# Low parts from PSUM, later prompt rows, adaLN sums on four column groups and attention outputs scaled during the scan: four edits to a one-layer diffusion step

## The chip, the cores and the metric

One core of one Trainium2 chip runs the whole step. Its engines are TensorE (PE; its weight loads stand apart as PEld), VectorE (DVE), ScalarE (ACT), GpSimd (POOL) and SyncE (SP, which here only issues transfers). The metric is the device time of one execution in microseconds; lower is better.

## The reference, cut to what matters

The layer works on 1024 latent tokens and 256 prompt tokens of width 1024:

```python
sh1, sc1, g1, sh2, sc2, g2 = split(silu(cond) @ w_ada + b_ada, 6)   # adaln, for c and for c_ctx
h = rms_norm(x, norm_mix_w) * (1.0 + sc1) + sh1
z = h @ w_in                      # hq, hf_f, hf_b, hi, hg, aq, ak, av, gl
o_a = softmax(q k^T) v            # 8 heads of 64, block by block; q, k normalised, rotary for latents
o_h = two gated recurrent scans (hgrn), forward and backward, 4 heads of 128
merged = g[0] * (o_h @ w_ho) + g[1] * (o_a @ w_ao)
x = x + g1 * (merged @ w_out)
h = rms_norm(x, norm_ffn_w) * (1.0 + sc2) + sh2
x = x + g2 * (square(relu(h @ w_ff1)) @ w_ff2)     # then a final rms_norm
```

Prompt tokens use the modulation of `c_ctx`, latent tokens that of `c`. All products are wanted in float32.

## The kernel before

**Products.** A float32 product is made of three matmuls: both operands are split into a high part (rounded to the format `fp32r`) and a low part (the rest), and high x high, high x low and low x high are summed in PSUM. ACT makes high parts, DVE makes low parts.

**Tiles.** Tokens come in three tiles `t`: 0 and 1 are latent (512 each), 2 is the prompt (256). The channels of the width come in 8 chunks `kc` of 128.

**Order.** PE's instructions run in the order in which the program writes them. For the other engines a scheduler orders the instructions by simulating the program, with priorities and with `issue_after` (not before a named instruction). Each engine, and SP's transfer queue too, then works strictly in its order.

**Stages.** Up to about 100 us is the front. It computes the first 16 of the 48 column chunks of the modulation (`front_ada`). `norm1_rows(t)` loads rows `xr` of x, squares and sums them (tile `sq` on ACT, `sqv` on DVE), makes the factor `rst` (on DVE tile `mm`, then a power on POOL) and scales the rows on DVE (`f(0)`, `f(1)`, L279). `norm1_tr` transposes them on PE into PSUM tile `ps_t` (L285). `norm1_col` applies the modulation: ACT writes the high part `hs` (L297); the full value `xnb` is made by ACT (L302), or by DVE where `kc % 3 == 1` (L300); DVE subtracts the high part from it to get the low part (L303). `front_z` (L644 to L650) multiplies with the weights of k, v and half of q, in 24 steps (t, kc) counted by `idx`. The transposes run some steps ahead of the products: the last ones of latent tile 1 and the first ones of the prompt stand side by side in PE's order.

Attention follows, from about 138 to 690 us. Between its blocks a filler `fz` feeds PE with groups of projections for the scan: ten groups, in two rounds `zh(0)` and `zh(1)` of hq, hf, hf, hi, hg. Then comes the scan (`hgrn`, to about 985 us; 24 units, `i` counts them) with a filler `fg` of eight groups for the merge gates, and then the transition: attention outputs `OA` and scan outputs `OH` are loaded again from DRAM (tile `or`), the attention outputs are multiplied with the reciprocal softmax sums (`RS`, loaded as broadcast rows, L1337), all are split (L313) and projected (L345 to L347). The rest, from about 1030 us, is the merge, the output projection and the feed-forward layers.

**The rest of adaLN.** The other 32 column chunks are computed two at a time beside the fillers. `ada_sum` lets POOL multiply and add the rows (into `ACC`, shown as `sums` and `pvt`), and PE then only sums over the partitions (L210); nine calls, one in each group of `fz` but the first. `ada_cols` does it all on PE in four column groups of 32 (L178), copies the sums by ACT into `ev` and transposes them (L184); seven calls in `fg`. PSUM tile `ps_t` has two buffers, which attention's transposes (L877) share; the weight tile `wraw` has two as well, and SP's ring of tiles (`or`, `xr` and the scan's loads among them) twenty.

Of the kernel before, what the change touches and what calls it, by code (L numbers as in the profile page):

```python
# [44 lines left out]
def build(ctx, tc, I, O, C):  # L45
# [147 lines left out]
    def ada_sum(ci, acc):  # L193

        raw = wraw(I["w_ada"], KC, ci * P)
        w = [ada_l[:, :, c:c + 1].broadcast_to([P, KC, 256]) for c in range(2)]
        g_.tensor_tensor(acc[0], raw[:, 0], w[0][:, 0], op=ALU.mult)
        for k in range(1, KC):
            g_.tensor_tensor(acc[1], raw[:, k], w[0][:, k], op=ALU.mult)
            g_.tensor_tensor(acc[0], acc[0], acc[1], op=ALU.add)  # L200
        g_.tensor_tensor(raw, raw, w[1], op=ALU.mult)
        for n in (4, 2):
            g_.tensor_tensor(raw[:, 0:n], raw[:, 0:n], raw[:, n:2 * n], op=ALU.add)
        g_.tensor_tensor(acc[1], raw[:, 0], raw[:, 1], op=ALU.add)

        def late():
            pt = PS("t")
            for b in range(2):
                for c in range(2):
                    pe.matmul(pt[:, 2 * c + b:2 * c + b + 1], acc[c][:, b * P:(b + 1) * P], ones, start=True, stop=True)  # L210
            with tc.high_priority(offset=600):
                v.tensor_tensor(modc[:, :, ci:ci + 2], pt[:, 0:4].rearrange("p (c b) -> p c b", c=2),
                                cols[:, B_ADA + ci:B_ADA + ci + 2].unsqueeze(1).broadcast_to([P, 2, 2]), op=ALU.add)
        return late


# [32 lines left out]
    def norm1_rows(t, blocks, xs, behind=None):  # L249

        t0, n, cond = TT[t]
        b0, nb = blocks[0], len(blocks)
        ss = T(8, "ss")
        rst = T(4, "rst")
        for b in blocks:
            xt = load_x(t0 // P + b)
            for i in range(2):
                acc = ss[:, 2 * (b - b0) + i:2 * (b - b0) + i + 1]
                with ExitStack() as after:
                    if behind:  # L260
                        for x in behind[b, i]:
                            after.enter_context(tc.issue_after(x.ins))
                    if i == 1:
                        jk = S(name="sqv")
                        v.scalar_tensor_tensor(jk, xt[i], 1.0, xt[i], op0=ALU.mult, op1=ALU.mult, accum_out=acc)
                    else:
                        jk = S(name="sq")
                        s_.activation(jk, xt[i], AF.Square, accum_out=acc)
            xs.append(xt)
        m = T(4, "mm")  # L270
        ssv = ss.rearrange("p (b i) -> p b i", i=2)
        v.tensor_tensor(m[:, 0:nb], ssv[:, 0:nb, 0], ssv[:, 0:nb, 1], op=ALU.add)
        v.tensor_scalar(m[:, 0:nb], m[:, 0:nb], 1.0 / D, EPS, op0=ALU.mult, op1=ALU.add)
        powed = g_.tensor_tensor(rst[:, 0:nb], m[:, 0:nb], mexp[:, 0:nb], op=ALU.pow)

        def scale(i):
            for b in blocks:
                x = xs[b][i]
                v.tensor_scalar(x, x, rst[:, b - b0:b - b0 + 1], None, op0=ALU.mult)  # L279
        return powed, scale  # L280
# [7 lines left out]
    def norm1_col(t, kc, pt, blocks=None):  # L288
        t0, n, cond = TT[t]
        if not blocks or blocks[0] == 0:  # L290
            hT[t][kc] = hpair(t)
        c = slice(blocks[0] * P, blocks[-1] * P + P) if blocks else slice(0, n)
        hi, lo = [x[:, c] for x in hT[t][kc]]
        pt, xn = pt[:, c], xnb[:, kc % 4, c]
        sc, sh = s1[:, cond, kc:kc + 1], modc[:, cond, kc:kc + 1]
        with tc.high_priority(offset=600):
            made = s_.activation(hi, pt, AF.Identity, scale=sc, bias=sh)  # L297

            if kc % 3 == 1 and t < 2:
                v.tensor_scalar(xn, pt, sc, sh, op0=ALU.mult, op1=ALU.add)  # L300
            else:
                s_.activation(xn, pt, AF.Identity, scale=sc, bias=sh)  # L302
            low[0] = v.tensor_tensor(lo, xn, f32(hi), op=ALU.subtract)  # L303
        return made

    low = [None]
# [391 lines left out]
            done += 1  # L698

    for idx in range(len(steps)):  # L700
        if idx > KC:
            ahead(idx + AHEAD + (idx > 11) + (idx > 13))
        t, kc = steps[idx]
# [35 lines left out]
        elif idx == KC:  # L739
# [4 lines left out]
                made = norm1_col(1, k, half[k], (2, 3))  # L744
            with tc.issue_after(made.ins):
                evs += front_done(0, banks0, (1,))
            _, f = norm1_rows(2, (0, 1), rows_n[2], {(b, i): [low[0] if i else made] for b in range(2) for i in range(2)})
            f(0)
            f(1)
            with tc.issue_after(loaded.ins):  # L750
                lbs = load_rest()
            with tc.issue_after(low[0].ins):
# [165 lines left out]
    def sums_rows():  # L918

        pt = PS("t")  # L920
        pe.transpose(pt[0:80, 0:P], rsum, ident)
        e = S((80, P), name="rT")
        s_.activation(e, pt[0:80, 0:P], AF.Copy)
        dma(RS, e)

    gone, keyed, copied = [None], [None], [None]
    q_at, o_at = {}, {}
# [260 lines left out]
    def hgrn(fill, before):  # L1188
# [11 lines left out]
            units[0].prep()  # L1200
        before()
        units[0].keys_t()
        for i in range(N + LATE):
            part = lambda x: fill.to((done + x * share[i]) / tot)
            if i + 1 < N:
                with ExitStack() as after:
                    after.enter_context(tc.issue_after(copied[0].ins))
                    after.enter_context(tc.issue_after(keyed[0].ins))
                    units[i + 1].prep()
            if i < N:  # L1210
                u = units[i]
                part(0.25)
# [39 lines left out]
    def with_ada(groups, ahead, behind):  # L1252

        late = []
        for i, grp in enumerate(groups):
            nxt = groups[i + 1] if i + 1 < len(groups) else None
            at, acts = 0.0, []
            if i and ahead:
                ci = ahead.pop(0)
                t0, t1 = (0.25, 0.9) if nxt else (0.02, 0.42)  # L1260
                acts = [(t0, lambda: late.append(ada_sum(ci, ACC))), (t1, lambda: late.pop()())]
            for need, n, gen in grp.stages():
                if not grp.tok and need == (0,):
                    jobs = [(0.5, lambda: grp.part(1))]
# [19 lines left out]
        if todo:  # L1284
            todo.pop()()

    fz = Filler(with_ada([*zh(0), *zh(1)], list(range(16, 34, 2)), []), 250.0)
    while pending:
        fz.add(1.0)
        flush(1.0)  # L1290
# [4 lines left out]
    gls = [Group(GL + 256 * c, gl_consume(c), False) for c in range(8)]  # L1295
    with tc.high_priority(offset=600):
        gls[0].part(0)
    fg = Filler(with_ada(gls, [], list(range(34, 48, 2))), 196.0)
    hgrn(fg, fz.rest)
    fg.rest()  # L1300
    close("sl")
# [24 lines left out]
    for t in MT:  # L1326
        n = TT[t][1]
        for c in range(8):
            r = S(name="or")
            dma(r[:, 0:n], (OH if c < 4 else OA)[c % 4][t])  # L1330
            if c >= 4:
                q = S(name="or")
                for i in range(2):
                    r0 = 10 * (2 * (c - 4) + i) + TT[t][0] // P
                    row = RS[r0:r0 + n // P, :].rearrange("(o b) p -> o (b p)", o=1)
                    dma(q[64 * i:64 * i + 64, 0:n], row.broadcast_to([64, n]))
                v.tensor_tensor(r[:, 0:n], r[:, 0:n], q[:, 0:n], op=ALU.mult)  # L1337
            oT[t][c] = hpair(t)
            split(oT[t][c][0], oT[t][c][1], r[:, 0:n])
    mg = [[None] * KC for _ in range(3)]  # L1340
# [676 lines left out]
```

## Time and profile before

| what | value |
|---|---|
| device time, median of three runs | 2040.8 us (2040.52 to 2042.02) |
| device time of the profiled execution | 2040.07 us |
| its span in the profile | 2038.3 us |
| granted TensorE clock, mean | 0.999 |
| PE busy | 2004.0 us (98%) |
| DVE, ACT, POOL busy | 1346.3, 940.0, 526.7 us |

The span is the time from the first to the last instruction of the profiled execution; its device time is 1.8 us longer. In the profile, busy is the time in which an engine had an instruction running. A wait row names the waiting engine and line, what ended the wait, the total, how often, and the longest. A row of the timeline gives start, duration, engine, line, output and input names, how many instructions it joins, and in brackets the idle time before it.

### The profile page before, as it was taken

What the parts mean: (1) busy time and instruction counts of PE and PEld (TensorE: products, weight loads), DVE (VectorE), ACT (ScalarE), POOL (GpSimd) and SP (SyncE); (2) the same over time, 40 slices, a digit from 0 to 9 for tenths busy, and PEclk for the clock granted to TensorE, in tenths of its full rate; (3) what the DMA queues carried; (4) which work ended last, traced back from release to release, by engine and by line L of the source; (5) the groups of instructions that cost most, each with busy time, mean ns of one, the idle gap of its engine ahead of it and who ended that gap; (6) DMA issues with size and microseconds to landing.
All of it is one profiled execution on the core that took longest, in us unless ns stands there. A gap on an engine that the chain in (4) does not pass through costs nothing.

```text
span 2038.3 us, 33049 instructions
## 1 busy us (share of the span) xinstructions
PE 2004.0 (98%) x12246; PEld 1734.4 (85%) x12246; DVE 1346.3 (66%) x2474; ACT 940.0 (46%) x1965; POOL 526.7 (26%) x594
## 2 busy tenths in 40 slices
PE   7899999999999999999999999999999999999998
PEld 5698889988889988888878889988888888888886
DVE  5865665655665789877355635886666666577786
ACT  4635555555565423323312335755545544333443
POOL 1471321433303655544022101222112200000120
PEclk9999999999999999999999999999999999999999
DMA  9452211322122455554844424854454489455764
GB/s 317 155 193 83 81 58 47 105 93 76 38 92 80 149 158 175 160 176 149 249 145 143 170 104 148 258 183 146 146 164 145 147 309 357 135 166 171 237 236 138
DMA packets 222626, 320.00 MB, mean 157 GB/s; under 512 B 19161, under 2 KB 140801, under 8 KB 222465
## 3 DMA queue, kind: packets, MB, share of 16 engines
q1 hardware_dynamic: 209984, 277.99, 42.8%
q0 software_dynamic: 12480, 39.91, 5.3%
q8 instruction: 96, 1.57, 0.3%
q14 instruction: 66, 0.53, 0.1%
HBM read 232.05 MB, written 85.78 MB: 156 GB/s over the span
## 4 chain that ended last, share of the span: by engine, by line
PE 90%; DMA 4%; DVE 3%; ACT 1%; issue 1%; SPq 0%; POOL 0%; POOLq 0%; DVEq 0%; ACTq 0%
PE ps_g L345 8%; PE ps_g L346 7%; PE ps_g L347 7%; PE ps_s L845 4%; PE ps_t L877 4%; PE ps_g L362 2%; PE ps_g L892 2%; PE ps_g L364 2%; PE ps_g L363 2%; PE ps_g L1804 2%; PE ps_g L1806 2%; PE ps_g L1805 2%; PE ps_g L891 2%; PE ps_s L1649 2%; PE ps_s L1651 2%; PE ps_s L1650 2%
## 5 line engine op out<-in xcount | busy, mean ns | idle before, releaser
L345 PE MATMUL ps_g<-hs,wsp 128*128 128x512 f32 (+1 forms) x896 | 322.6, 360 | 0.0
L346 PE MATMUL ps_g<-hs,wsp 128*128 128x512 f32 (+1 forms) x896 | 309.2, 345 | 2.9 <-DVE hs L313 2.9
L347 PE MATMUL ps_g<-hs,wsp 128*128 128x512 f32 (+1 forms) x896 | 309.3, 345 | 0.0
L312 ACT ACTIVATE wsp<-wraw 128x512 fp32r<-128x512 f32 (+1 forms) x186 | 116.7, 668 | 208.4 <-PE ps_g L346 81.2
L846 DVE TENSOR_REDUCE mx<-ps_s 128x1 f32<-128x512 f32 (+1 forms) x208 | 138.1, 668 | 112.6 <-PE ps_s L845 110.6
L880 DVE TENSOR_TENSOR pTl<-ps_t,pTh 128x512 fp32r<-128x512 f32 x200 | 136.4, 684 | 88.0 <-ACT pTh L880 87.6
L313 DVE TENSOR_TENSOR wsp<-wraw,wsp 128x512 fp32r<-128x512 f32 (+1 forms) x186 | 147.4, 817 | 70.0 <-ACT wsp L312 69.7
L347 PEld LDWEIGHTS ps_g<-hs,wsp 128*128 128x128 f32 x896 | 169.3, 189 | 21.7
L345 PEld LDWEIGHTS ps_g<-hs,wsp 128*128 128x128 f32 x896 | 169.6, 189 | 20.3 <-issue 4.4
L346 PEld LDWEIGHTS ps_g<-hs,wsp 128*128 128x128 f32 x896 | 169.9, 190 | 18.2 <-DVE hs L313 3.4
L880 ACT ACTIVATE pTh<-ps_t 128x512 fp32r<-128x512 f32 x200 | 118.2, 602 | 139.3 <-PE ps_t L877 137.6
L312 ACT ACTIVATE ah<-ar 128x640 fp32r<-128x640 f32 (+1 forms) x112 | 80.9, 723 | 185.9 <-PE ps_g L1805 102.3
L857 ACT ACTIVATE pexp<-ps_s,ngm 128x512 f32<-128x512 f32 (+1 forms) x208 | 137.4, 669 | 42.7 <-DVE ngm L850 42.3
L313 DVE TENSOR_TENSOR ah<-ar,ah 128x640 fp32r<-128x640 f32 (+1 forms) x112 | 92.0, 822 | 78.2 <-ACT ah L312 77.8
L845 PE MATMUL ps_s<-Kl,Ql 128*128 128x512 f32 (+1 forms) x416 | 129.5, 411 | 0.0
L877 PE MATMUL ps_t<-ident,pexp 128*128 128x128 f32 x800 | 120.0, 272 | 0.1
L362 PE MATMUL ps_g<-wsp,hs 128*128 128x256 f32 x400 | 115.8, 289 | 0.0
L364 PE MATMUL ps_g<-wsp,hs 128*128 128x256 f32 x400 | 112.9, 282 | 0.0
L363 PE MATMUL ps_g<-wsp,hs 128*128 128x256 f32 x400 | 112.6, 281 | 0.0
L892 PE MATMUL ps_g<-pTl,Vl 128*128 128x256 f32 x400 | 104.2, 283 | 0.2
L891 PE MATMUL ps_g<-pTh,Vl 128*128 128x256 f32 x400 | 104.0, 281 | 0.0
L877 PEld LDWEIGHTS ps_t<-ident,pexp 128*128 128x128 f32 x800 | 94.4, 140 | 9.5 <-issue 0.6
(436 smaller groups left out, 5363.0 us busy)
## 6 DMA issues: line engine op xcount, KB each, us to landing
ar<-AF SPq DMA_DIRECT2D x112, 320.0 KB, 3.3
wraw<-in_w_ff SPq DMA_DIRECT2D x32, 1024.0 KB, 6.4
wr<-in_w_ff SPq DMA_DIRECT2D x128, 256.0 KB, 4.4
wraw<-in_w_in SPq DMA_DIRECT2D x18, 1024.0 KB, 5.6
wraw<-in_w_ada SPq DMA_DIRECT2D x16, 1024.0 KB, 5.4
AF<-a POOLq DMA_DIRECT2D x48, 256.0 KB, 2.7
AF<-t POOLq DMA_DIRECT2D x48, 256.0 KB, 2.3
wa<-in_w_ada SPq DMA_DIRECT2D x32, 256.0 KB, 5.9
```

The costliest lines, as they stand in the source:

```text
L312: s_.activation(hi, raw, AF.Copy)
L313: return v.tensor_tensor(lo, raw, f32(hi), op=ALU.subtract)
L345: pe.matmul(out, hi[:, k, :], mh, start=(first and k == 0), stop=False)
L346: pe.matmul(out, hi[:, k, :], ml, start=False, stop=False)
L347: pe.matmul(out, lo[:, k, :], mh, start=False, stop=(last and k == kcs - 1))
L362: pe.matmul(po[:, bb, :], mh[:, off:off + P], wh[:, k % 4, :], start=(k == 0), stop=False)
L363: pe.matmul(po[:, bb, :], mh[:, off:off + P], wl[:, k % 4, :], start=False, stop=False)
L364: pe.matmul(po[:, bb, :], ml[:, off:off + P], wh[:, k % 4, :], start=False, stop=(k == KC - 1))
L845: pe.matmul(pq[:, 0:n], self.qh[:, q0:q0 + P], K[self.g][var][self.kts[i]], start=(var == 0), stop=(var == 1))
L877: pe.transpose(pt[:, a, j * P:(j + 1) * P], self.Ps[j][i][:, b * P:(b + 1) * P], ident)
L880: behind[:] = s_.activation(hi, pt, AF.Copy), v.tensor_tensor(lo, pt, f32(hi), op=ALU.subtract)
L892: pe.matmul(pv[:, 0:256], V[self.g][kg][:, b, :], lo[:, a, :], start=False, stop=(k == last))
```

## The change

Four places are edited.

1. `ada_sum`: the sum over partitions is made with a column of ones, broadcast to 32 columns, as the stationary operand and the sums as the moving one, in four column groups of one PSUM tile; ACT copies the result to `ev`, and a second step (`last`) transposes it and adds the bias. `with_ada` now places two calls in each hi and hg group (`grp.tok`) but the last, and one in every other group but the first: twelve calls in `fz` and four `ada_cols` calls in `fg`, in place of nine and seven.
2. `norm1_col`: where DVE made `xnb`, it now computes `pt * sc - hi` from PSUM and then adds `sh`, so that the low part is the second instruction's result and waits for ACT's high part earlier.
3. Prompt rows: `norm1_rows(2)` moves from `idx == KC` to `idx == KC + 2`, all four squares of the prompt go to ACT, and the scaling is held until after the latest low part.
4. `scale_pair`: the twelve multiplies with `RS`, their loads, and a store of the result to `OA`, stand in the scan's loop: loads in odd rounds `i > 2`, multiply and store in the next even one. The transition then loads `OA` and splits it.

What the edits do to the order of the engines is shown at three places. Line numbers are those of each kernel's own file; in the changed one the squares are L274, the high part L303, `xnb` L309, the new sums L209 and their transpose L215.

The prompt rows on ACT. Before, in the front, at latent tile 1 (`sq` of `xr` is a prompt square, `hs` a high part; the other two squares are on DVE):

```order
L268 ACTIVATE sq,ss<-xr 128x512
L297 ACTIVATE hs<-ps_t,modc,s_119 128x512
L302 ACTIVATE xnb<-ps_t,modc,s_119 128x512
L268 ACTIVATE sq,ss<-xr 128x512
L514 ACTIVATE vst<-kve 128x2x64 x4
L297 ACTIVATE hs<-ps_t,modc,s_119 128x512
L302 ACTIVATE xnb<-ps_t,modc,s_119 128x512
```

The two squares stand ahead of the high parts of columns 2 and 3 of latent tile 1. After, where latent tile 1 ends and the prompt begins (`hs` of 128x512 is the last latent high part, `hs` of 128x256 the first of the prompt):

```order
L303 ACTIVATE hs<-ps_t,modc,s_119 128x512
L309 ACTIVATE xnb<-ps_t,modc,s_119 128x512
L274 ACTIVATE sq,ss<-xr 128x512 x2
L303 ACTIVATE hs<-ps_t,modc,s_119 128x512
L274 ACTIVATE sq,ss<-xr 128x512 x2
L303 ACTIVATE hs<-ps_t,modc,s_119 128x256
L309 ACTIVATE xnb<-ps_t,modc,s_119 128x256
```

All four squares moved behind the `xnb` of column 6, two of them also behind the high part of column 7, the last latent one.

The sums of adaLN on PE, in a group of `fz` during attention. Before (`sums` and `pvt` hold the products added by POOL and are the weights here, the column `ones` is what moves):

```order
L346 MATMUL ps_g<-hs,wsp 128x512
L347 MATMUL ps_g<-hs,wsp 128x512
L210 MATMUL ps_t<-ones,sums 128x1
L210 MATMUL ps_t<-ones,pvt 128x1
L210 MATMUL ps_t<-ones,sums 128x1
L210 MATMUL ps_t<-ones,pvt 128x1
L345 MATMUL ps_g<-hs,wsp 128x256
L346 MATMUL ps_g<-hs,wsp 128x256
```

After, the four matmuls, and further on the transpose of ACT's copy `ev`:

```order
L354 MATMUL ps_g<-hs,wsp 128x256
L209 MATMUL ps_t<-sums,ones 32x128 x2
L209 MATMUL ps_t<-pvt,ones 32x128 x2
L900 MATMUL ps_g<-pTh,Vl 128x256
L901 MATMUL ps_g<-pTl,Vl 128x256
```

```order
L353 MATMUL ps_g<-hs,wsp 128x256
L354 MATMUL ps_g<-hs,wsp 128x256
L215 MATMUL ps_t<-ident,ev 128x128
L352 MATMUL ps_g<-hs,wsp 128x256
L353 MATMUL ps_g<-hs,wsp 128x256
L354 MATMUL ps_g<-hs,wsp 128x256
```

Four matmuls with one moving column gave way to four with 32 columns of weights and 128 moving columns, and the transpose stands twenty rows later, behind attention and group work.

The transfers on SP, at the start of the transition. Before (`or<-OA` loads an attention output, `or<-RS` one half of its broadcast factors):

```order
L101 DMA or<-OH_0_1731 128x512
L101 DMA or<-OA_0_1710 128x512
L101 DMA or<-RS 64x512 x2
L101 DMA or<-OA_0_1713 128x512
L101 DMA or<-RS 64x512 x2
L101 DMA or<-OA_0_1716 128x512
L101 DMA GT_1_1827<-ze 128x512
L101 DMA OH_2_1733<-oT 128x256
L101 DMA or<-RS 64x512 x2
L101 DMA or<-OA_0_1719 128x512
L101 DMA or<-RS 64x512
```

After, at the same place, and one pair of the scan's loop:

```order
L101 DMA or<-OH_0_1731 128x512
L101 DMA or<-OA_0_1710 128x512
L101 DMA or<-OA_0_1713 128x512
L101 DMA or<-OA_0_1716 128x512
L101 DMA or<-OA_0_1719 128x512
L101 DMA or<-OH_2_1724 128x256
L101 DMA GT_0_1826<-ze 128x512
```

```order
L101 DMA or<-OA_1_1711 128x512
L101 DMA or<-RS 64x512 x2
L101 DMA GT_1_1815<-ze 128x512
L101 DMA uf<-FD_3_1_1773 128x512
L101 DMA uq<-QD_1_1749 128x512
L101 DMA OA_2_1721<-or 128x256
L101 DMA uv<-VD_1_1779 128x4x128
L101 DMA GT_2_1816<-ze 128x256
```

The broadcast loads left the transition; in the scan they and the store `OA<-or` stand between the scan's own loads (`uf`, `uq`, `uv`) and the filler's stores (`GT<-ze`).

```diff
@@ ada_sum
         def late():
-            pt = PS("t")
-            for b in range(2):
-                for c in range(2):
-                    pe.matmul(pt[:, 2 * c + b:2 * c + b + 1], acc[c][:, b * P:(b + 1) * P], ones, start=True, stop=True)
-            with tc.high_priority(offset=600):
-                v.tensor_tensor(modc[:, :, ci:ci + 2], pt[:, 0:4]...
+            pa = PS("t")
+            for q in range(4):
+                pe.matmul(pa[32 * q:32 * q + 32, 0:P], ones.broadcast_to([P, 32]), acc[q // 2][:, (q % 2) * P:(q % 2 + 1) * P], start=True, stop=True)
+            ev = S((P, P), name="ev")
+            s_.activation(ev, pa[:, 0:P], AF.Copy)
+
+            def last():
+                pt = PS("t")
+                pe.transpose(pt[:, 0:P], ev, ident)
+                with tc.high_priority(offset=600):
+                    v.tensor_tensor(modc[:, :, ci:ci + 2], pt[:, 0:P]...
+            return last
         return late
@@ norm1_rows
-                    if i == 1:
+                    if i == 1 and t < 2:
                         jk = S(name="sqv")
@@ norm1_col
             if kc % 3 == 1 and t < 2:
-                v.tensor_scalar(xn, pt, sc, sh, op0=ALU.mult, op1=ALU.add)
+                v.scalar_tensor_tensor(xn, pt, sc, f32(hi), op0=ALU.mult, op1=ALU.subtract)
+                low[0] = v.tensor_scalar(lo, xn, sh, None, op0=ALU.add)
             else:
                 s_.activation(xn, pt, AF.Identity, scale=sc, bias=sh)
-            low[0] = v.tensor_tensor(lo, xn, f32(hi), op=ALU.subtract)
+                low[0] = v.tensor_tensor(lo, xn, f32(hi), op=ALU.subtract)
@@ the front's steps
     for idx in range(len(steps)):
+        if idx == KC + 2:
+            _, f = norm1_rows(2, (0, 1), rows_n[2], {(b, i): [made] for b in range(2) for i in range(2)})
+            with tc.issue_after(low[0].ins):
+                f(0)
+                f(1)
...
-            _, f = norm1_rows(2, (0, 1), rows_n[2], {(b, i): [low[0] if i else made] for b in range(2) for i in range(2)})
-            f(0)
-            f(1)
@@ new, beside the attention
+    def scale_pair(c, t):
+        n = TT[t][1]
+        r, q = S(name="or"), S(name="or")
+        dma(r[:, 0:n], OA[c][t])
+        for i in range(2):
+            r0 = 10 * (2 * c + i) + TT[t][0] // P
+            row = RS[r0:r0 + n // P, :].rearrange("(o b) p -> o (b p)", o=1)
+            dma(q[64 * i:64 * i + 64, 0:n], row.broadcast_to([64, n]))
+        def late():
+            v.tensor_tensor(r[:, 0:n], r[:, 0:n], q[:, 0:n], op=ALU.mult)
+            dma(OA[c][t], r[:, 0:n])
+        return late
@@ hgrn
+        pairs, scaled = [(c, t) for t in (0, 2, 1) for c in range(4)], []
         for i in range(N + LATE):
+            if i > 2 and i % 2 and pairs:
+                scaled.append(scale_pair(*pairs.pop(0)))
...
+            if scaled and i % 2 == 0:
+                with tc.issue_after(keyed[0].ins):
+                    scaled.pop()()
@@ with_ada
-                ci = ahead.pop(0)
-                t0, t1 = (0.25, 0.9) if nxt else (0.02, 0.42)
-                acts = [(t0, lambda: late.append(ada_sum(ci, ACC))), (t1, lambda: late.pop()())]
+                def begin():
+                    late.append(ada_sum(ahead.pop(0), ACC))
+                def end():
+                    late.append(late.pop()())
+                acts = [(0.02, begin), (0.45, end), (0.49, lambda: late.pop()())] if grp.tok else []
+                if nxt:
+                    acts += [(0.5 if grp.tok else 0.25, begin), (0.93, end), (0.97, lambda: late.pop()())]
@@ the two fillers
-    fz = Filler(with_ada([*zh(0), *zh(1)], list(range(16, 34, 2)), []), 250.0)
+    fz = Filler(with_ada([*zh(0), *zh(1)], list(range(16, 40, 2)), []), 250.0)
-    fg = Filler(with_ada(gls, [], list(range(34, 48, 2))), 196.0)
+    fg = Filler(with_ada(gls, [], list(range(40, 48, 2))), 190.0)
@@ the transition
             dma(r[:, 0:n], (OH if c < 4 else OA)[c % 4][t])
-            if c >= 4:
-                q = S(name="or")
-                for i in range(2):
-                    ...
-                    dma(q[64 * i:64 * i + 64, 0:n], row.broadcast_to([64, n]))
-                v.tensor_tensor(r[:, 0:n], r[:, 0:n], q[:, 0:n], op=ALU.mult)
```

More of the change, by code (lines that the diff above doesn't have):

```diff
@@ L206, in late @@
         def late():
-            pt = PS("t")
-            for b in range(2):
-                for c in range(2):
-                    pe.matmul(pt[:, 2 * c + b:2 * c + b + 1], acc[c][:, b * P:(b + 1) * P], ones, start=True, stop=True)
-            with tc.high_priority(offset=600):
-                v.tensor_tensor(modc[:, :, ci:ci + 2], pt[:, 0:4].rearrange("p (c b) -> p c b", c=2),
-                                cols[:, B_ADA + ci:B_ADA + ci + 2].unsqueeze(1).broadcast_to([P, 2, 2]), op=ALU.add)
+            pa = PS("t")
[7 more added lines that the diff above has]
+                with tc.high_priority(offset=600):
+                    v.tensor_tensor(modc[:, :, ci:ci + 2], pt[:, 0:P].rearrange("p (c b x) -> p c b x", c=2, b=2)[:, :, :, 0],
+                                    cols[:, B_ADA + ci:B_ADA + ci + 2].unsqueeze(1).broadcast_to([P, 2, 2]), op=ALU.add)
+            return last
         return late
@@ L1330, in build @@
             dma(r[:, 0:n], (OH if c < 4 else OA)[c % 4][t])
-            if c >= 4:
-                q = S(name="or")
-                for i in range(2):
-                    r0 = 10 * (2 * (c - 4) + i) + TT[t][0] // P
-                    row = RS[r0:r0 + n // P, :].rearrange("(o b) p -> o (b p)", o=1)
-                    dma(q[64 * i:64 * i + 64, 0:n], row.broadcast_to([64, n]))
-                v.tensor_tensor(r[:, 0:n], r[:, 0:n], q[:, 0:n], op=ALU.mult)
             oT[t][c] = hpair(t)
```

## The prediction

> **What bounds the kernel now.** I read the page first (span, busy time, chain), then the windows, then PE's own waits, and last the timeline of each place that the change touches.
>
> ```profile
> span 2038.3 us, 33049 instructions
> ...
> PE 2004.0 (98%) x12246; PEld 1734.4 (85%) x12246; DVE 1346.3 (66%) x2474; ACT 940.0 (46%) x1965; POOL 526.7 (26%) x594
> ...
> PE 90%; DMA 4%; DVE 3%; ACT 1%; issue 1%; SPq 0%; POOL 0%; POOLq 0%; DVEq 0%; ACTq 0%
> ```
>
> PE is busy for 98% of the span and carries 90% of the chain. So the time falls only by less work on PE or by filling one of its gaps. The windows (stretch, its length, then busy time of PE, PEld, DVE, ACT, POOL) tell where gaps are:
>
> ```profile
> 50.00:60.00 10.00, 8.30 (x43) 6.17 (x41) 7.51 (x21) 6.61 (x18) 0.75 (x1) 1.00 0.42 137
> 60.00:70.00 10.00, 7.95 (x39) 6.16 (x40) 9.51 (x29) 8.60 (x21) 2.56 (x3) 1.00 0.65 211
> 70.00:80.00 10.00, 8.54 (x45) 6.61 (x43) 9.80 (x18) 5.22 (x10) 8.60 (x7) 1.00 0.23 70
> ...
> 200.00:700.00 500.00, 499.06 (x3529) 461.14 (x3528) 305.14 (x580) 289.16 (x688) 160.59 (x166) 1.00 0.24 79
> 700.00:800.00 100.00, 100.00 (x843) 84.33 (x842) 90.73 (x198) 31.39 (x74) 57.04 (x58) 1.00 0.54 170
> 800.00:990.00 190.00, 189.21 (x1573) 162.42 (x1572) 138.93 (x343) 60.13 (x161) 86.42 (x96) 1.00 0.54 169
> 1000.00:1030.00 30.00, 26.14 (x141) 22.27 (x140) 20.09 (x39) 15.01 (x32) 0.76 (x1) 1.00 0.74 225
> ```
>
> Attention and scan leave PE about 1.7 us of gaps in 790. The front lacks 5.2 us between 50 and 80 us, where DVE reaches 95 to 98%, and the transition lacks 3.9 us. PE's waits name what ends them:
>
> ```profile
> PE ps_t L285 <- ACT xnb L302: 4.0, 4, 1.4
> PE ps_g L346 <- DVE hs L313: 2.9, 2, 2.1
> PE ps_s L346 <- DVE hs L313: 0.9, 1, 0.9
> PE ps_s L1122 <- POOL usf L1073: 0.8, 1, 0.8
> PE ps_t L210 <- DVE pTl L880: 0.7, 2, 0.4
> PE ps_t L285 <- DVE kT L313: 0.5, 1, 0.5
> PE ps_t L285 <- DVE qT L313: 0.3, 1, 0.3
> ```
>
> **Sums of adaLN.** This is work on PE itself, so its whole price counts. The timeline of PE gives an old call, a call of the column-group form, and the transpose of that form:
>
> ```profile
> 537.38 0.28 PE L210 MATMUL ps_t<-ones,sums 128*128 128x1 f32 x2
> ...
> 538.18 0.36 PE L891 MATMUL ps_g<-pTh,Vl 128*128 128x256 f32 x1
> 538.39 0.28 PE L892 MATMUL ps_g<-pTl,Vl 128*128 128x256 f32 x1
> 538.51 0.28 PE L891 MATMUL ps_g<-pTh,Vl 128*128 128x256 f32 x1
> ...
> 740.01 1.08 PE L178 MATMUL ps_g<-wraw,ada_l 128*32 128x128 f32 x32
> 741.02 0.50 PE L345 MATMUL ps_g<-hs,wsp 128*128 128x512 f32 x1
> 741.36 0.40 PE L346 MATMUL ps_g<-hs,wsp 128*128 128x512 f32 x1
> ...
> 992.22 0.47 PE L345 MATMUL ps_g<-hs,wsp 128*128 128x512 f32 x1
> 992.53 0.39 PE L346 MATMUL ps_g<-hs,wsp 128*128 128x512 f32 x1
> ```
>
> I count from start to start. An old call takes 0.80 us (537.38 to 538.18), and the matmul behind it 0.21 where the one after takes 0.12, so 0.89 in all; nine make 8.0. An `ada_cols` call is 32 passes in 1.01, 0.032 each, and the matmul behind it takes 0.34 where twice 0.12, 0.23, is usual: 0.11. On entering I estimate 0.09, as the old call lost on leaving; its transpose costs 0.11 (the row behind it takes 0.31 for 0.23, and the transpose 0.03). That is 1.32, and three calls go: 4.0. A new call is 8 passes of the form just shown: 8 x 0.032 = 0.25, with 0.09, 0.11 and 0.11 around it 0.56; twelve make 6.7. Net 6.7 - 8.0 - 4.0 = -5.3.
>
> [...]
>
> Each new call takes a `ps_t` buffer twice, the first until ACT has copied. Before, nine such takings cost 0.7 us, 0.08 each; 24 make 1.9, so +1.2. The bounds: 0.0 each (-0.7) and the longest, 0.4, each (+8.9). I stay near the mean because PE runs on for twenty rows between the two. Sum of this part: **-4.1** (-6.0 to +3.6). On POOL a call is a stretch of 20 us:
>
> ```profile
> 141.10 0.91 POOL L197 TENSOR_TENSOR sums<-wraw,ada_l 128x256 f32<-128x256 f32 x1 [0.29 <-DMA wraw<-in_w_ada]
> ...
> 160.31 0.73 POOL L204 TENSOR_TENSOR pvt<-wraw 128x256 f32<-128x256 f32 x1
> ```
>
> Three more are 60 us of POOL, which is busy for only 161 of the 500 between 200 and 700; they lie beside PE. Ten groups in the 552 us of attention are some 55 us each, and a call has 0.43 of one, about 24 us: enough, with little to spare; a late sum would hold PE, and attention with it, by what is missing. DVE's add moves with its call. ACT's twelve copies lie in its idle time (211 of the 500 us); a late one is the wait for `ps_t` just priced.
>
> **Front.** The rows of PE with waits, a prompt square, the prompt scaling, and DVE's and POOL's groups there:
>
> ```profile
> 53.59 0.73 PE L650 MATMUL ps_g<-wraw,hs 128*128 128x512 f32 x2 [0.37 <-DVE hs L303]
> ...
> 63.27 0.66 PE L285 MATMUL ps_t<-ident,xr 128*128 128x128 f32 x4 [0.69 <-ACT xnb L302]
> ...
> 67.51 0.66 PE L285 MATMUL ps_t<-ident,xr 128*128 128x128 f32 x4 [0.84 <-DVE xnb L300]
> ...
> 70.77 0.82 PE L285 MATMUL ps_t<-ident,xr 128*128 128x128 f32 x6
> ...
> 58.37 0.67 ACT L268 ACTIVATE sq<-xr 128x512 f32<-128x512 f32 x1
> ...
> 64.19 1.67 DVE L279 TENSOR_SCALAR xr<-xr,rst 128x512 f32<-128x512 f32 x4
> ...
> L303 DVE TENSOR_TENSOR hs<-xnb,hs 128x512 fp32r<-128x512 f32 x8 | 5.5, 689 | 0.5 <-ACT xnb L302 0.5
> L300 DVE TENSOR_SCALAR xnb<-ps_t,s,modc 128x512 f32<-128x512 f32 x3 | 2.4, 804 | 0.0
> L493 POOL TENSOR_TENSOR qb<-qn,sinb 128x512 f32<-128x512 f32 x2 | 2.7, 1350 | 1.0 <-DVE qn L481 1.0
> L274 POOL TENSOR_TENSOR rst<-mm,mexp 128x2 f32<-128x2 f32 x3 | 2.3, 790 | 48.1 <-DVE mm L272 35.9 <-DVE mm L273 12.2
> ```
>
> The gain: two squares (0.67 each) leave ACT and two (the same work) leave DVE in the stretch from 58 to 61 us. The low part of a DVE column goes from 0.80 + 0.69 to 0.80 and a one-source instruction, which like the scaling (1.67 / 4) is 0.42. I take back the 0.37 and the 0.84, and 0.54 of the 0.69: 1.75, so the transposes of column 7 start at 69.0 in place of 70.77. The longest wait, 1.4 near 60 us, I leave, since ACT's high part there follows the transposes at once.
>
> The loss: the six transposes at 70.77 are four of column 7 and two of the prompt's column 0, one behind the other. The prompt's rows were scaled at 65.9, 5 us ahead of need. After, from 69.0: transposes 0.5, the last latent high part 0.7, the two squares behind it 1.3, two short sums on DVE 0.3, POOL's power 0.8, three of four scalings 1.25, handovers 0.2: the prompt's transposes start at 74.05, before at 71.2. All PE work behind them waits along, 2.85 us. Of the later waits those for kT (0.5) and qT (0.3) hang on work that goes on meanwhile, and go. Net **+2.0**. Bounds: with the squares ahead of the last high part (-1.3) and all later waits absorbed (0.8, and 1.9 of the 4.0 for `xnb`) the net is -1.2; with POOL's power behind a long rotary product (1.35, the row of `qb`) and nothing absorbed, +4.2. On SP the prompt's row loads move behind a few loads of constants; the rows are first read near 67 us in place of 58.4, which covers it, and a late row would lengthen PE's wait by as much.
>
> **Transition.** The rows are DVE's wait and a multiply:
>
> ```profile
> DVE or L1337 <- DMA or<-RS: 26.9, 10, 8.6
> ...
> 1019.31 0.69 DVE L1337 TENSOR_TENSOR or<-or 128x512 f32<-128x512 f32 x1 [6.37 <-DMA or<-RS]
> ```
>
> DVE's low parts of `or` stood behind multiplies that waited for broadcast loads; those waits and the loads go. PE lost 2.9 + 0.9 = 3.8 there to exactly these low parts. What is late next is the plain load of `OA` in a stretch where the DMA engines are 74% busy, so I keep 0.8: **-3.0** (-3.8 to 0).
>
> **Scan.** Twelve multiplies of at most 0.69 are 8.3 us more for DVE, over some 260 us in which it is busy for 73 to 91% and PE loses 0.8. The scan's products reach PE with slack, so I take **+0.5**; bounds -0.4 and, were every multiply to stand in PE's way, +8.3.
>
> **Sum.** -4.1 + 2.0 - 3.0 + 0.5 = -4.6. The profiled execution, 2040.07, is 0.7 under the median of 2040.8; from the median I get 2036.2 and forecast **2036**. A measurement of this kernel tells about 0.2%, 4.1 us, from no change: faster means under 2036.7.
>
> **Rivals.**
> - *Front and transition give it back.* POOL's power comes late (+4.2 in place of 2.0) and the transition stays bound by DMA (-0.8 in place of -3.0). For: 74% DMA, DVE at 98% from 70 to 80 us. Against: the broadcast loads, as many bytes as the outputs that they scale, are gone. 2036.2 + 4.4 = 2040.6: no change.
> - *Slower: SP's order in the scan.* The store `OA<-or` cannot be issued until its multiply is done, and the scan's loads `uf`, `uq`, `uv` stand behind it in the same queue. For: DVE at 91% from 700 to 800 us. Against: only 0.8 us of waits in the scan so far. Each of twelve stores that holds PE by 1.0 us costs 12, giving 2047.7; it decides from 0.8 us a store on.
> - *Waits for ps_t.* At 0.4 for each of 24 takings the sum is 7.7 higher, 2043.9. For: attention's transposes share both buffers. Against: 0.08 is the mean.
> - *The one-column sums were cheap already,* and what 0.80 shows is the way around them: at an old call of 0.34 (8 x 0.032 and 0.09) nine are 3.1, the sum is 4.9 higher, 2041.1. The spacing of the rows speaks against it. [...]
> - *The front gains.* At -1.2 in place of 2.0 the time is 2033.0. For: the squares may be issued in another order of time than I replayed. Against: the order on ACT as written.
>
> **Chances.** Forecast 0.50 (its own range 2034 to 2038.5, two thirds of it under 2036.7), back to no change 0.20, the front gains 0.12, SP's order 0.07, `ps_t` 0.06, cheap sums 0.05. Faster: 0.34 + 0.12 = 0.46; same: 0.16 + 0.20 + 0.05 = 0.41; slower: 0.13. The range from 2032 to 2043 leaves out the two slow cases and the ends of the others.
>
> **What would show it.** The new sums (L209) should take about 0.25 us from first to last start, and their transposes leave no wait. In the front I look for the transposes of the prompt's column 0 near 74 us with a wait of 4 to 5 us for DVE's scaling, and none at 67.5. In the transition PE's wait for DVE's low parts under 1 us. In the scan no new wait for `uf` or for the low parts. The forecast fails if the prompt's wait is far from 4.6 us, if waits for `ps_t` in attention pass 3 us, or if PE waits in the scan.

## The result, and the profile after

The changed kernel takes 2061.3 us (median of four runs, 2059.55 to 2063.37), the kernel before 2041.4 in the same runs: ratio 1.0095, 95% interval [1.0077, 1.0112], slower by about 20 us. Forecast was 2036. In the medians of this document three executions of over 2850 us, at a granted clock of 0.66 or less, are left out, the profiled one of mul_only among them. The profiled execution after took 2063.37 us, that of before 2040.07. The page's lines that answer to those shown of before:

```profile
span 2061.4 us, 33065 instructions
...
PE 2009.1 (97%) x12183; PEld 1733.6 (84%) x12183; DVE 1340.5 (65%) x2467; ACT 944.4 (46%) x1978; POOL 583.2 (28%) x651
...
PE 50%; DVE 3%; DMA 2%; issue 1%; ACT 1%; SPq 0%; POOLq 0%; ACTq 0%; DVEq 0%
```

The page has 63 instructions of PE fewer, but PE lost time in gaps and, in places, at a lower clock. The chain's shares of after add up to 57% only: it breaks off within the span, so the places are found by windows and by marks in time. The windows of after (stretch, length, busy time of PE, PEld, DVE, ACT, POOL, then granted clock, DMA share, GB/s):

```profile
70.00:80.00 10.00, 2.50 (x9) 1.82 (x8) 8.30 (x16) 3.13 (x8) 5.63 (x5) 0.62 0.26 81
80.00:90.00 10.00, 8.81 (x40) 7.07 (x39) 3.48 (x6) 3.82 (x8) 1.29 (x1) 0.87 0.23 79
200.00:700.00 500.00, 499.57 (x3548) 456.18 (x3548) 306.13 (x579) 294.79 (x707) 213.33 (x218) 1.00 0.26 83
700.00:800.00 100.00, 94.28 (x811) 81.27 (x809) 82.85 (x182) 28.06 (x63) 52.94 (x53) 1.00 0.54 169
800.00:990.00 190.00, 179.67 (x1401) 151.99 (x1402) 144.78 (x360) 56.10 (x144) 90.53 (x101) 0.97 0.52 166
1000.00:1030.00 30.00, 30.00 (x163) 25.86 (x162) 4.64 (x10) 7.87 (x20) 0.71 (x1) 1.00 0.74 238
```

Against before, PE's busy time from 70 to 80 us fell from 8.54 to 2.50, the scan lost 5.7 and 9.5 us in its two windows, and the transition has no gap left (the stretch from 1030 to 1060 us is full as well). PE's waits after:

```profile
PE ps_s L1158 <- issue: 12.3, 5, 5.1
PE ps_t L291 <- DVE xr L285: 7.8, 2, 7.5
PE ps_t L1135 <- DVE uf L1097: 3.4, 3, 1.3
PE ps_t L291 <- DVE qT L320: 1.5, 2, 1.2
```

L1158 is the scan's product with `uv`, L1135 the scan's transposes of `uf`, L291 the transposes of the front. Where the time went can be read from the first and last starts of the same products in both traces:

| point | before | after | later by |
|---|---|---|---|
| first attention score | 157.3 | 165.3 | 8.0 |
| last product with V in attention | 689.0 | 697.1 | 8.1 |
| last product of the scan with `uv` | 974.8 | 1001.1 | 26.3 |
| first product of the first feed-forward layer | 1340.8 | 1363.0 | 22.2 |
| span | 2038.3 | 2061.4 | 23.1 |

So the front lost 8.0 us, attention nothing, the scan 18.2; the transition gained 4.1, and the last 0.9 lie in the feed-forward layers and the end.

**The front.** The timeline of after, with PE's wait, ACT's squares, DVE's queue behind them and POOL's power:

```profile
69.58 0.60 PE L291 MATMUL ps_t<-ident,xr 128*128 128x128 f32 x4
77.68 0.78 PE L291 MATMUL ps_t<-ident,xr 128*128 128x128 f32 x2 [7.50 <-DVE xr L285]
78.11 0.77 PE L651 MATMUL ps_g<-wsp,hs 128*128 128x512 f32 x1
78.68 0.63 PE L652 MATMUL ps_g<-wsp,hs 128*128 128x512 f32 x1
79.11 0.63 PE L651 MATMUL ps_g<-wsp,hs 128*128 128x512 f32 x1
...
72.17 0.19 ACT L274 ACTIVATION_READ_ACCUMULATOR sq<-xr 128x1 f32 x1
...
72.60 0.74 DVE L306 SCALAR_TENSOR_TENSOR xnb<-ps_t,s,hs 128x512 f32<-128x512 f32 x1
73.26 0.89 DVE L488 TENSOR_TENSOR qn<-qe,qrst 128x512 f32<-128x512 f32 x1
74.07 0.48 DVE L307 TENSOR_SCALAR hs<-xnb,modc 128x512 fp32r<-128x512 f32 x1
74.47 1.49 DVE L501 TENSOR_TENSOR qa<-qa,qb 128x256 f32<-128x256 f32 x1
75.88 0.15 DVE L278 TENSOR_TENSOR mm<-ss 128x2 f32<-128x2 f32 x1
77.04 1.68 DVE L285 TENSOR_SCALAR xr<-xr,rst 128x512 f32<-128x512 f32 x4 [0.81 <-POOL rst L280]
...
74.23 1.45 POOL L500 TENSOR_TENSOR qb<-qn,sinb 128x512 f32<-128x512 f32 x1 [0.63 <-DVE qn L488]
76.31 0.69 POOL L280 TENSOR_TENSOR rst<-mm,mexp 128x2 f32<-128x2 f32 x1 [0.64 <-DVE mm L279]
```

The last square is read out at 72.36, but DVE gets to the sum `mm` only at 75.88: four instructions, 3.5 us, stand ahead of it in its queue. PE waits 7.50, and its products then start 0.43 us apart in place of 0.23, up to 82.5 us: the granted clock is 0.62 and 0.87 in these windows.

**The scan.** Timeline of SP, DVE and PE near 790 us, and rows of SP's and DVE's waits in the scan:

```profile
786.11 0.32 SPq L101 DMA_DIRECT2D or<-OA  x1
788.62 0.48 SPq L101 DMA_DIRECT2D or<-RS  x1
...
790.37 0.51 SPq L101 DMA_DIRECT2D uf<-FD  x1
790.99 0.37 SPq L101 DMA_DIRECT2D uq<-QD  x1
791.79 0.32 SPq L101 DMA_DIRECT2D OA<-or  x1
796.32 0.56 SPq L101 DMA_DIRECT2D uv<-VD  x1
...
794.93 1.22 DVE L1075 TENSOR_TENSOR_SCAN ucp<-R,uf 128x512 f32<-128x512 f32 x1 [4.54 <-DMA uf<-FD]
...
799.62 0.72 DVE L1167 SCALAR_TENSOR_TENSOR ust<-ust,udec,ps_s 128x128 f32<-128x128 f32 x2
...
800.44 1.83 PE L1158 MATMUL ps_s<-uv,ukt 128*128 128x128 f32 x7 [4.38 <-issue]
...
SPq L101 <- DMA OA<-or: 11.9, 3, 4.1
...
DVE ucp L1071 <- DMA uf<-FD: 16.0, 7, 4.5
DVE ucp L1075 <- DMA uf<-FD: 15.9, 5, 4.8
DVE uq L1115 <- DMA uq<-QD: 7.5, 3, 3.6
```

SP issues nothing for 5.3 us before the pair's load `or<-OA` at 786.11, and for 2.2 before `or<-RS`; the scan's `uf` stands behind them and is issued at 790.37. DVE's scan waits 4.54 us for it. SP then issues the store `OA<-or` at 791.79 and the next load, `uv`, only at 796.32; three such waits for a store to land cost SP 11.9 us.

PE could start its product at 796.06 and starts it at 800.44. The row calls this wait "issue" and names no releaser. `uv` has landed by 799.76, and DVE's L1167, which reads a `ps_s` tile, ends at 800.34. PE's two other waits of over 2 us at L1158 also end some 0.1 us after a DVE instruction that reads `ps_s` (at 887.75 after L1167, at 950.16 after L1190), the last of them 4.1 us after its `uv` had landed. So what PE waits for is, by these times, DVE, and DVE is late by its loads: it waits 39.4 us for `uf` and `uq` in the scan, where a kernel without the pairs there (noscale, below) has 3.1.

**The sums.** The four new matmuls on PE, with the rows around them:

```profile
692.98 0.28 PE L371 MATMUL ps_g<-wsp,hs 128*128 128x256 f32 x1
693.19 0.30 PE L209 MATMUL ps_t<-sums,ones 128*32 128x128 f32 x2
...
693.55 0.39 PE L369 MATMUL ps_g<-wsp,hs 128*128 128x256 f32 x1
693.77 0.28 PE L370 MATMUL ps_g<-wsp,hs 128*128 128x256 f32 x1
```

From 692.98 to 693.77 are 0.79 us, of which two products at 0.12 are 0.24: the call takes 0.55, and 0.66 with its transpose, where 0.56 was forecast. No wait at it or its transpose is in the trace.

### The profile page after: what moved, and what is told of

The parts are those of the page before. It is cut to its first block, busy times and chain, and to the rows that moved or that the text cites. A ratio compares the mean times of both kernels' runs of the same rounds, so it can differ in the third digit from the quotient of the medians.

```text
span 2061.4 us, 33065 instructions
## 1 busy us (share of the span) xinstructions
PE 2009.1 (97%) x12183; PEld 1733.6 (84%) x12183; DVE 1340.5 (65%) x2467; ACT 944.4 (46%) x1978; POOL 583.2 (28%) x651
## 4 chain that ended last, share of the span: by engine, by line
PE 50%; DVE 3%; DMA 2%; issue 1%; ACT 1%; SPq 0%; POOLq 0%; ACTq 0%; DVEq 0%
PE ps_g L352 3%; PE ps_g L353 3%; PE ps_g L354 3%; PE ps_g L1834 2%; PE ps_g L1833 2%; PE ps_g L1832 2%; PE ps_s L1677 2%; PE ps_s L1679 2%; PE ps_s L1678 2%; PE ps_s L1834 2%; PE ps_s L1833 2%; PE ps_s L1832 2%; PE ps_t L1833 2%; PE ps_t L1832 2%; PE ps_t L1834 2%; PE ps_t L1679 1%
## 5 line engine op out<-in xcount | busy, mean ns | idle before, releaser
L320 DVE TENSOR_TENSOR wsp<-wraw,wsp 128x512 fp32r<-128x512 f32 (+1 forms) x186 | 151.7, 839 | 95.7 <-ACT wsp L319 95.4
```

Source lines behind the costliest of these rows:

```text
L320: return v.tensor_tensor(lo, raw, f32(hi), op=ALU.subtract)
```

## The experiments

The kernel before ran between 2042.3 and 2042.8 (medians) beside all of them, and at 2041.4 beside the changed kernel. Ratios are to it; a difference to the changed kernel's 2061.3 is uncertain by the 1.3 us between the two.

**The pairs back in the transition (noscale).**

```diff
-        pairs, scaled = [(c, t) for t in (0, 2, 1) for c in range(4)], []
+        pairs, scaled = [], []
@@ the transition: loads of RS and multiplies as before
```

> The changed kernel with the twelve multiplies and their loads back in the transition. Between the markers of the two traces the scan lost 18 us and the transition gained 4. Theory (the extra transfers in SP's order hold the scan's loads): the scan's loss goes and the transition's gain too, 2061.3 - 18 + 4 = 2047; no wait of PE for uv (L1158) longer than 1 us. Rival (the scan suffers from the moved sums of adaLN, not from the multiplies): 2061 to 2065, with waits as before.

2044.64 us, ratio 1.0008 [0.9998, 1.0017]. The theory holds: 16.7 us come back. The stretch from attention's last product to the scan's last is 281.5 us with the pairs out and 304.0 with them in, so they cost the scan 22.5. PE's waits at L1158 and L1135, 12.3 and 3.4, are 15.7 of it; most of the rest is the clock of 0.97, by an estimate 0.03 of 190 us, 5.7. From there to the feed-forward layer it is 367.6 against 361.9, so the transition gained 5.7 by them. The kernel before needs 366.0 there.

**The prompt's rows back (noprompt).**

```diff
-        if idx == KC + 2:
-            _, f = norm1_rows(2, ...)          # and squares 0 and 1 of each row on ACT and DVE again
...
+            _, f = norm1_rows(2, (0, 1), rows_n[2], {(b, i): [low[0] if i else made] for b in range(2) for i in range(2)})
```

> The changed kernel with the prompt's rows where they were (before the weights' last columns, two squares on DVE). Theory (PE's wait of 7.5 us for the prompt's scaling and the low clock behind it make the front's loss of 8 us): 2061.3 - 8 = 2053, granted clock 1.00 from 70 to 90 us. Rival (the new form of the low parts loads DVE so that it is late anyway): at most 3 us back, 2058 or more.

2054.25, ratio 1.0056 [1.0041, 1.0071]: 7.1 us back, as the theory has it. But in the traces only 5.0 of them lie in the front (the first score is at 160.3 for 165.3), and the scan is 4.5 shorter too (299.5 for 304.0). The first score is still 3 us later than before; a wait for qT is new (below).

**Both out (neither):** the two edits above together.

> Only the sums of adaLN on four column groups and the new low parts stay. Theory (the two losses are independent): 2041.4 with -1.75 in the front and -4 for the sums, 2036 to 2038. Rival (the sums wait for the two buffers of ps_t): 2041 or more, with waits of PE at L209 or L886.

2041.04, ratio 0.9992 [0.9983, 1.0002]: neither the 2037 of the theory nor the rival's waits. PE's waits show what is left in the front:

```profile
PE ps_t L291 <- DVE qT L320: 3.5, 2, 3.2
PE ps_t L291 <- ACT xnb L309: 2.9, 3, 1.4
PE ps_t L291 <- DVE xnb L306: 2.1, 2, 1.4
```

With the new low parts alone, the transposes of the prompt's columns wait 3.2 us for DVE's low part of qT. Noprompt is this kernel with the pairs in the scan: it takes 13.2 us more, and its scan 299.5 for 281.3. So the pairs cost the scan 18.2 us here and 22.5 beside the later prompt rows; why the two differ is not shown.

**The sums alone (ada_only):** neither, with the old low parts too.

> The kernel before with the sums of adaLN alone changed. Theory (the new sums save their 4 us of PE, and what the front loses comes from the low parts): 2041.4 - 4.2 = 2037, the front's first attention score at 157 us. Rival (the sums cost what they save through waits for ps_t): 2041.

2037.57, ratio 0.9972 [0.9962, 0.9983]: 5.2 us under before, the sums' forecast and a little more. So the new low parts cost 3.5 us (2041.04 against 2037.57), not the gain that I gave them.

**The prompt's move without the low parts (ada_prompt):** the sums and the move.

> The new sums of adaLN and the later prompt rows, with the low parts as before and no pairs in the scan. Theory (the prompt's wait of 7.5 us is made by the move itself): 2037.6 + 6 to 9 = 2044 to 2047, first attention score 6 to 9 us later than the 158 of the kernel with the sums alone. Rival (the move loses only together with the new low parts): 2037 to 2040.

2045.89, ratio 1.0020 [1.0010, 1.0030]: the move alone costs 8.3 us, with a wait of 8.72 for the scaling. With the low parts as well (noscale) it is 7.1: the two share their loss, and do not add.

**New low parts for latent tile 0 alone (ada_low0).**

```diff
-            if kc % 3 == 1 and t < 2:
+            if kc % 3 == 1 and t == 0:      # t == 1 keeps xnb and its subtraction
```

> The new sums of adaLN, and the new low parts for latent tile 0 alone. Theory (the new low parts lose where DVE is full, in latent tile 1): 2036.5 to 2037.6, no wait of 3 us for qT. Rival (they lose in either tile): 2040.

2038.7, ratio 0.9982 [0.9972, 0.9991]. The time is 1.1 us over the theory's range, but the wait of 3 us for qT is gone, so it was tile 1 that made it; a gain over the sums alone does not show (the intervals overlap).

**Work for PE in the wait (busy_wait):** noscale, and

```diff
+            if (t, kc) == (2, 0):
+                pt0 = PS("t")
+                for _ in range(40):
+                    pe.transpose(pt0[:, 256:256 + P], ident, ident)
```

> The changed kernel without the pairs (2044.6) and with forty more transposes, of the identity, on PE ahead of the prompt's first column, where PE idles 7.5 us. They take some 4.5 us of that wait. Theory (the idle time itself lowers the granted clock, and the products behind it run at half speed for 4 to 5 us): the wait shrinks to about 3 us, the granted clock from 80 to 90 us is 1.00, and the front is 2 to 3 us shorter although PE does more, 2042. Rival (the clock falls for another reason): same time, clock 0.6 to 0.9 from 70 to 90 us.

2044.4, ratio 1.0012 [1.0002, 1.0021]; the median is that of noscale. The windows of this kernel:

```profile
70.00:80.00 10.00, 6.86 (x50) 6.00 (x49) 7.76 (x16) 2.77 (x7) 5.09 (x5) 1.00 0.25 80
80.00:90.00 10.00, 8.81 (x48) 7.15 (x47) 4.07 (x7) 4.80 (x11) 1.29 (x1) 1.00 0.23 79
```

and PE's row:

```profile
77.04 0.72 PE L291 MATMUL ps_t<-ident,xr 128*128 128x128 f32 x2 [3.08 <-DVE xr L285]
```

The wait is 3.08, the clock 1.00, and the first score stands at 162.7 where noscale has 165.0. Of these 2.3 us 0.37 are there already when the prompt's transposes start (77.04 for 77.41); the other 1.9 arise behind them. So in the profiled executions the theory holds and the low clock costs 1.9 us. The medians do not resolve it. Behind the changed kernel's wait of 7.50 us the granted clock is 0.50 from 78 to 82 us, and products stand 0.43 apart for 0.23. But after the 3.2 us wait for qT the window from 80 to 90 us shows a clock of 0.66 in one kernel (neither) and 1.00 in the other (noprompt), and after a wait of 2.47 us in the changed kernel's scan (at 887.75) the granted clock is 0.50 from 889 to 890 us: it has been low after shorter waits too, and how long a wait must be for that no run here shows.

**The store on POOL's queue (pool_store).**

```diff
-            dma(OA[c][t], r[:, 0:n])
+            store(OA[c][t], r[:, 0:n])
```

> The changed kernel with the store of the scaled attention output issued on POOL's queue in place of SP's. Theory a (the store waits on SP for its multiply and the scan's loads stand behind it): scan back by 8 to 15 us, 2046 to 2053. Theory b (the buffers of the ring of twenty are held by the pair until the store has landed, whatever the queue): 2057 to 2063. Theory c (DVE's extra work): 2060 to 2063.

2057.63, ratio 1.0074 [1.0057, 1.0091]: 3.7 us back, but this interval and the changed kernel's overlap, and the scan's 299.8 us are no fewer than noprompt's 299.5 with the store on SP. SP still waits 12.7 us for the store to land. The store's place on SP is the smaller part at most.

**Multiplies alone (mul_only):** noscale, and in the scan twelve multiplies of `R` with itself, without a transfer.

> The changed kernel with the transition as before and, in the scan, twelve multiplies of the same sizes on a tile that lies in SBUF anyway: no loads, no stores, no tile of the ring of twenty. Theory of the transfers: the scan keeps its length without the pairs, 2044.6 plus at most 2. Theory of DVE (its 8 us more make the scan's chain late): scan 240 to 245 us between its first key transpose's products, 2061 to 2066.

2044.75 (median of nine), ratio 1.0010 [1.0000, 1.0019]: 0.1 us over noscale. DVE's work is not the cause.

**Loads and store without the multiply (load_only); loads and multiply without the store (load_mul).** The transition is as before in both.

```diff
-            v.tensor_tensor(r[:, 0:n], r[:, 0:n], q[:, 0:n], op=ALU.mult)     # load_only
...
-            dma(OA[c][t], r[:, 0:n])                                          # load_mul
```

> The changed kernel with the transition as before and, in the scan, the pairs' loads and the store of the attention output as it was loaded, without the multiply. Theory of the transfers and their buffers: the scan loses 15 to 22 us, 2060 to 2067. Theory of DVE: 2044.6 plus at most 3.

> The changed kernel with the transition as before and, in the scan, the pairs' loads and multiplies, without the store of the product. Theory a (the buffer held until the store has landed is what the scan's loads wait for): 2044.6 plus 5 to 8, as with the loads and the store alone. Theory b (a multiply that waits in DVE's order for its loads, which themselves wait for buffers, closes the loop): 2060 or more even without the store.

2050.25, ratio 1.0036 [1.0022, 1.0049], and 2053.91, 1.0066 [1.0047, 1.0086]: 5.6 and 9.3 us over noscale. The first lies between its two theories, the second 1.3 above theory a (its four executions spread from 2052.3 to 2061.0). The parts, 0.1, 5.6 and 9.3, stay far below the whole, 22.5. In the traces the time from a pair's load to its store, on the mean of twelve, is 5.8 us in load_only and 25.5 in the changed kernel; in load_mul 24.3 pass from the load to the end of the multiply. So the buffers are held far longer once a multiply stands between, but that alone does not make the whole: load_mul holds them nearly as long and costs less than half.

**Halves in one buffer of their own (j_half):** twenty pairs of 256 columns, both parts in one idle buffer, stored on POOL's queue.

> The changed kernel with the pairs cut into twenty halves that use one buffer of their own (not the ring of twenty), stored on POOL's queue. Theory of the ring's buffers: the scan's waits for uv go, 2061.3 - 16 = 2045, or 2040 to 2048. Theory of SP's order alone: 2055 to 2060, as with the store moved. Theory of DVE: 2060 or more, since twenty of 0.42 are as much.

2055.41, ratio 1.0060 [1.0040, 1.0080]. It tells the theories apart badly, since SP now waits for this one buffer, 69.2 us in all.

```profile
SPq L101 <- DMA OA<-ojk: 69.2, 15, 8.7
```

It does show that no buffer of the ring need be taken: the scan has 293.9 us, 12.4 more than in noscale, with SP's queue held up like this and DVE waiting 8.4 us for the halves' own loads.

**A ring of eighteen without pairs (ring18).** The sums alone, and

```diff
-RINGS = {"X": 20,
+RINGS = {"X": 18,
```

> The kernel with the new sums alone (2037.6), and the ring of twenty buffers cut to eighteen: no pair, no transfer, no multiply added. Theory of the buffers (the scan's loads run only as far ahead as the ring lets them, and it has none to spare): scan longer by 5 us or more, 2043 to 2055, with waits of DVE for uf and of PE for uv. Theory of SP's order: at most 2 us, 2037 to 2040. Attention uses the ring too and could lose a little in either.

2036.47, ratio 0.9976 [0.9967, 0.9986]. My theory of a ring without a spare buffer falls: two fewer cost nothing.

**Eighteen, and two for the pair (own_ring); the factors outside the ring (q_j).**

```diff
+RINGS = {"X": 18, ..., "Y": 2}                                    # own_ring
+        r, q = S(name="or", ring="Y"), S(name="or", ring="Y")     # own_ring
...
+        r, q = S(name="or"), S(name="ojk")                        # q_j: a buffer idle in the scan
```

> The changed kernel with the ring cut to eighteen and a ring of two for the pair. Theory of the buffers: as the same kernel with eighteen left for the scan, no better than 2055. Theory of SP's order: 2061. If eighteen turn out to be enough (the run above), and the hold of the pair's buffers is the cause: 2045 to 2050.

> The changed kernel with the pair's factors in a buffer outside the ring, which lies idle in the scan; the attention output stays in the ring. Theory of the buffers: about half of the scan's 22 us back, 2048 to 2054. Theory of SP's order: 2059 to 2063.

2048.3, ratio 1.0032 [1.0019, 1.0045], and 2048.65, 1.0039 [1.0024, 1.0054]: 13.0 and 12.7 us under the changed kernel; the scan's stretch is 291.0 and 288.9 us for 304.0. So the number of buffers was not short: the pair's tiles among the ring's make the greater part of the loss, and with one of the two elsewhere that part is gone. SP's waits fit (by the program's ring a load that follows 20 tiles later waits for the store of the tile in its place, and 11.9 us of the changed kernel's waits end when a pair's store lands), but the order of buffers itself is not in a trace.

**A third of the pairs (scale4, scale4_qj).** The sums alone, and the four pairs of latent tile 1 in the scan.

```diff
+        pairs, scaled = [(c, 1) for c in range(4)], []
+            if i % 6 == 5 and pairs:
...
+            if scaled and i % 6 == 0:
@@ scale4_qj only
+        r, q = S(name="or"), S(name="ojk")
```

> The kernel with the new sums alone, and only the four pairs of latent tile 1, the ones whose low parts PE waits for in the transition, moved into the scan, one in every sixth round. If the scan absorbs them: 2037.6 - 3 = 2034.6. If each costs what one of the twelve did (22 / 12 = 1.9): 2037.6 + 7.5 - 3 = 2042.

> The new sums of adaLN and the four pairs of latent tile 1 in the scan, with the pair's factors in the buffer outside the ring. Theory of the buffers: most of the scan's 3 us come back, 2036.4 - 2 = 2034.4 or 2033.5 to 2035.5. If what is left is the transfers on SP: 2036.4.

2036.4, ratio 0.9973 [0.9963, 0.9982], and 2033.51, ratio 0.9957 [0.9944, 0.9971]. The last is the lowest median of all, 8.9 us under the kernel before; against scale4 and the sums alone the intervals overlap. Its windows show the gain in the transition with the scan nearly full:

```profile
700.00:800.00 100.00, 99.79 (x846) 85.11 (x846) 90.40 (x199) 31.41 (x74) 56.03 (x57) 1.00 0.59 182
800.00:990.00 190.00, 188.08 (x1481) 160.31 (x1480) 139.13 (x341) 59.62 (x158) 85.94 (x97) 1.00 0.55 170
1000.00:1030.00 30.00, 30.00 (x157) 25.66 (x156) 20.99 (x38) 16.18 (x35) 3.53 (x3) 1.00 0.51 166
```

**The scan in all traces.** The stretch from attention's last product to the scan's last, and DVE's waits for `uf` and `uq` from 700 to 1000 us:

| kernel | scan, us | DVE's waits, us |
|---|---|---|
| before | 285.8 | 5.3 |
| noscale | 281.5 | 3.1 |
| scale4_qj, scale4 | 283.4, 284.5 | 5.7, 6.8 |
| load_only, q_j | 287.2, 288.9 | 17.9, 18.3 |
| own_ring | 291.0 | 25.9 |
| load_mul | 292.5 | 30.0 |
| j_half | 293.9 | 23.6 |
| noprompt, pool_store | 299.5, 299.8 | 32.6, 34.4 |
| after | 304.0 | 39.4 |

But for j_half, and for the kernel before, whose scan has three `ada_cols` calls more, the two rise together: the longer DVE waits for the scan's loads, the longer the scan.

## Why the prediction was wrong, step by step

| term | forecast | measured | from |
|---|---|---|---|
| sums of adaLN | -4.1 | -5.2 | ada_only against before |
| front (low parts and prompt) | +2.0 | +7.1 | noscale against ada_only |
| transition | -3.0 | -4.1 to -5.7 | markers, after against before and noscale |
| scan | +0.5 | +22.5 | markers, after against noscale |

- **Scan: the step that failed.** "Twelve multiplies of at most 0.69" priced the pairs as DVE work, and that price was not too low: the multiplies alone cost 0.1. What failed is "The scan's products reach PE with slack, so I take +0.5": I set no price on the pairs' 48 loads and stores in SP's in-order queue, nor on the two buffers that each pair holds while it waits for loads, a multiply in DVE's queue and a store's landing. The scan's `uf` and `uq` came late by them, DVE waited 39.4 us for them in place of 3.1, and PE behind DVE: +22.5. The prediction's own sign for this stage, "no new wait for `uf`", tells it. The rival named SP's order, gave it 0.07, and 1.0 us a store; 22.5 / 12 is 1.9 a pair. It had the place and the sign right, and its mechanism only in part: 3.7 us, not clear of the intervals, went with the store's place on SP, 13.0 with the pair's buffers.
- **Front: the size.** The wait's cause and place were as described, at 77.7 in place of 74.05, since "two short sums on DVE 0.3" left out what stands ahead of them: DVE takes 3.5 us to come to them. The profile before told it: DVE at 98% from 70 to 80 us. The rival for the front named POOL's power, but POOL stands idle for 0.64 us before it. The second omission is the clock, some 1.9 us in the traces. The low parts, which were to help to a gain of 1.75, cost 3.5 by themselves, by a later qT.
- **Transition: right, too small.** The 0.8 kept for the loads did not come: PE has no gap there, and the stretch is 361.9 us in all eight kernels that move pairs into the scan. In those that leave them it varies from 363.8 to 368.3, so the gain is known only to some 2 us.
- **Sums: right, in part by luck.** A call is 0.66 for 0.56 (its eight passes take 0.36, from 693.19 to 693.55, for 0.25), which is 1.2 too much for twelve; its waits for `ps_t` are nil where 1.2 was added, so two misses offset each other. In the traces attention is as long as before (531.9 us in ada_only for 531.7), and the gain is the scan's, 281.3 for 285.8: the three `ada_cols` calls that went. POOL kept its time: it is busy 213 us from 200 to 700, for 161.

What stays open: with the pair's buffers out of the ring the scan still loses 9.5 us (291.0 against 281.5), and DVE still waits 25.9 us for its loads. The order on SP, where the pairs' transfers stand between the scan's, is argued from the waits and not tried by itself; j_half comes nearest and mixes it with a buffer of its own.

## What to carry to other kernels

Work moved under another stage can cost that stage more than its engine time (here 22.5 us, where the multiplies alone cost 0.1): count the buffers that it takes from a shared ring and how long each is held, from the load's issue to the store's landing, every load that queues behind, and the engine that waits for these loads. A chain moved later must be priced through the queue of each engine that it visits: DVE, at 98% there before, came to two instructions of 0.15 and 0.17 us 3.5 us late. And a part that gains alone (the sums) is worth measuring apart from those that it came with.

## What the runs showed of the hardware that I had not expected

A wait of PE had a price beyond its length here: after 7.5 us of idling, products ran at 0.43 us apart in place of 0.23 for about 4.4 us. In the scan of the changed kernel a granted clock of 0.50 followed waits of 2.47, 4.38 and 5.12 us (from 889 to 890, 801 to 806 and 951 to 952 us), and the mean from 800 to 990 us was 0.97. After waits of 3.2 us it went either way (1.00 in noprompt, 0.66 in neither, from 80 to 90 us). And a DVE sum of 128x256, 0.41 us before (at 73.27), took 1.49 after (L501 above) and ended 0.28 us behind a product of 128x512 that POOL ran beside it (L500). What held it up no run here shows.
